# The last 15 of 63 full loads through GpSimd's queue in a row-mean kernel

## The chip, the cores and the metric

The kernel runs on one core of one Trainium2 chip. The metric is the time of one execution on the device in microseconds; three timed runs of the kernel before gave 1243.21, 1243.28 and 1243.29 us. The profile is of one execution, and its span runs from the first to the last instruction.

## The reference

The input `x` has 64 x 256 x 8192 float32 numbers, 536.9 MB. The result is the mean over the last axis, 64 x 256 numbers:

```python
def reference(x):
    return np.mean(x, axis=2)
```

Each of the 16384 rows of 8192 numbers is summed and multiplied by 1/8192. Every number is read once, and almost nothing is written.

## The kernel before

The 16384 rows lie as 128 partitions with 128 rows each. The rows are cut into three zones of 95, 17 and 16 rows per partition (`ZONE`, L27); within a zone a partition owns consecutive rows, so a partition's part of a load is one stretch of memory. A full load takes two rows of each partition, 128 x 16384 numbers or 8 MiB, 64 KB for each partition. There are 63 of them (`NB`, L30), numbered g = 0 to 62; load 0 comes in three pieces. A last pair of rows is the tail: it comes in five chunks that become smaller (`cuts`, L42).

Three buffers of 8 MiB (`bufs`, L67) are used in turn: load g goes to buffer g mod 3. For each buffer there is a semaphore that counts landings (`in_sems`) and one that counts reductions done (`free_sems`). The engines do this:

- SP (`nc.sync`, from L102) issues every transfer, all through its one hardware queue. After the first three loads it runs a loop of 15 rounds of three (`ROUNDS`, L116 to L121): wait until the buffer's reduction is done, issue the load into it. That covers loads 3 to 47. Loads 48 to 62 (L122 to L125) are written out with the same wait. At L126 SP waits until load 60 is reduced, since the tail uses buffer 0, and issues the five chunks (L128 to L131). At the end it writes the results out (L133 to L138).
- DVE (`nc.vector`, from L145) waits for a buffer's landing and sums its two rows with one `tensor_reduce` (L166, in a loop of 20 rounds of three, loads 0 to 59; L176, loads 60 and 61). Load 62 and the tail's first chunk are summed by the helper `halves` (L147 to L158), which adds the two halves of a row and sums the result in one pass; of the chunks DVE sums a part, then adds all the parts of the last row (L197).
- ACT (L200 to L205) sums the other part of the first four chunks.
- GpSimd, POOL in the profile (L87 to L99), clears one cell at the start and multiplies the finished sums by 1/8192 once load 62 and the first chunk are summed.

The order of the loads in SP's queue is the order in which DVE sums them, and no more than three loads can be out or unread at a time.

Of the kernel before, what the change touches and what calls it, by code (L numbers as in the profile page):

```python
# [11 lines left out]
def bass_global_avg_pool_1d_kernel(  # L12
    nc: bass.Bass,
    x: bass.AP,
    out: bass.AP,
):
    P = 128
    ALIGN = 4096
    B, C, L = x.shape
    rows = B * C  # L20
    inv = 1.0 / float(L)

    OWN = rows // P
    ZONE = [95, 17, 16]  # L27
    FROM = [0, ZONE[0], ZONE[0] + ZONE[1]]
    EARLY, LATE = FROM[2], ZONE[2]
    NB = OWN // 2 - 1  # L30
    NBUF = 3
    PAIRS0 = ZONE[0] // 2
    ROUNDS = PAIRS0 // NBUF
    assert rows % P == 0 and sum(ZONE) == OWN and NB % NBUF == 0
    assert ZONE[0] % 2 == 1 and ZONE[1] % 2 == 1
    assert (PAIRS0 + 1) % NBUF == 0 and NB - PAIRS0 - 1 > NBUF
    LOADS0 = (NB - PAIRS0 - 1) // NBUF
    first_row = lambda g: 2 * g - 2 if g <= PAIRS0 else 2 * g
    FIRST = L // 4


    U = L // 256  # L42
    cuts = [0, L + 29 * U, L + 169 * U, L + 217 * U, L + 240 * U, 2 * L]
    mine = [29 * U, 50 * U, 17 * U, 8 * U]
    LAST = cuts[5] - cuts[4]
    NPART = 8

    flat = x.rearrange("b c l -> (b c) l")
    out_flat = out.rearrange("b c -> (b c)")
    zone = [  # L50
        flat[P * f : P * (f + n), :].rearrange("(p r) l -> p (r l)", p=P)
        for f, n in zip(FROM, ZONE)
    ]
    out_zone = [
        out_flat[P * f : P * (f + n)].rearrange("(p r) -> p r", p=P)
        for f, n in zip(FROM, ZONE)
    ]

    with ExitStack() as ctx:
        sb = lambda n, s: ctx.enter_context(nc.sbuf_tensor(n, s, F32))  # L60
        sem = lambda n: ctx.enter_context(nc.semaphore(n))
        res = sb("res", [P, OWN - 1])
        scaled = sb("scaled", [P, EARLY])
        ends = sb("ends", [P, LATE])
        fin = sb("fin", [P, LAST + NPART])
        sb("pad", [P, (-nc.sbuf_base % ALIGN) // 4])
        bufs = [sb(f"buf{i}", [P, 2 * L]) for i in range(NBUF)]  # L67

        in_sems = [sem(f"in_sem{i}") for i in range(NBUF)]
        free_sems = [sem(f"free_sem{i}") for i in range(NBUF)]  # L70
        first_sem = sem("first_sem")
        mixed_sem = sem("mixed_sem")
        chunk_sems = [sem(f"chunk_sem{c}") for c in range(5)]
        owned_sem = sem("owned_sem")
        part_d = sem("part_d")
        part_a = sem("part_a")
        pool_sem = sem("pool_sem")
        late_sem = sem("late_sem")
        out_sem = sem("out_sem")
        end_sem = sem("end_sem")  # L80

        tail = bufs[0]
        part = lambda n: fin[:, LAST + n : LAST + n + 1]

        eng = nc.gpsimd  # L87
        eng.memset(part(NPART - 1), 0.0).then_inc(part_d, 1)  # L88
        eng.wait_ge(free_sems[0], LOADS0 + 1)
        eng.wait_ge(owned_sem, 4)  # L90
        for dst, src in [
            (scaled[:, 0 : ZONE[0] - 1], res[:, 2 : ZONE[0] + 1]),
            (scaled[:, ZONE[0] - 1 : ZONE[0] + 1], res[:, 0:2]),
            (scaled[:, ZONE[0] + 1 : EARLY], res[:, ZONE[0] + 1 : EARLY]),
            (ends[:, 0 : LATE - 1], res[:, EARLY : OWN - 1]),
        ]:
            eng.tensor_scalar(dst, src, inv, None, op0=mybir.AluOpType.mult).then_inc(  # L97
                pool_sem, 1
            )  # L99


        eng = nc.sync  # L102
        def rows_of(n, k):
            z = 2 if n >= FROM[2] else 1 if n >= FROM[1] else 0
            return zone[z][:, (n - FROM[z]) * L : (n - FROM[z] + k) * L]

        a, z = rows_of(ZONE[0] - 1, 1), rows_of(ZONE[0], 1)
        eng.dma_start(bufs[0][:, 0:FIRST], a[:, 0:FIRST]).then_inc(first_sem, 16)
        eng.dma_start(bufs[0][:, FIRST:L], a[:, FIRST:L]).then_inc(mixed_sem, 16)
        eng.dma_start(bufs[0][:, L : 2 * L], z).then_inc(in_sems[0], 16)  # L110
        for g in range(1, NBUF):
            eng.dma_start(bufs[g][:], rows_of(first_row(g), 2)).then_inc(in_sems[g], 16)
        src = rows_of(first_row(NBUF), ROUNDS * NBUF * 2).rearrange(
            "p (i b w) -> b p i w", i=ROUNDS, b=NBUF
        )
        with eng.Fori(0, ROUNDS) as i:  # L116
            for b in range(NBUF):
                eng.wait_ge(free_sems[b], 1).then_inc(free_sems[b], -1)
                eng.dma_start(bufs[b][:], src[b][:, bass.ds(i, 1), :]).then_inc(
                    in_sems[b], 16  # L120
                )  # L121
        for g in range(PAIRS0 + 1, NB):  # L122
            b = g % NBUF
            eng.wait_ge(free_sems[b], (g - PAIRS0 - 1) // NBUF + 1)
            eng.dma_start(bufs[b][:], rows_of(first_row(g), 2)).then_inc(in_sems[b], 16)  # L125
        eng.wait_ge(free_sems[0], LOADS0 + 1)  # L126
        two = rows_of(2 * NB, 2)
        for c in range(5):  # L128
            a, z = cuts[c], cuts[c + 1]
            dst = tail[:, a:z] if c < 4 else fin[:, 0:LAST]  # L130
            eng.dma_start(dst, two[:, a:z]).then_inc(chunk_sems[c], 16)  # L131
        eng.wait_ge(pool_sem, 4)
        for z in range(2):  # L133
            eng.dma_start(
                out_zone[z], scaled[:, FROM[z] : FROM[z] + ZONE[z]]
            ).then_inc(out_sem, 16)
        eng.wait_ge(late_sem, 1)
        eng.dma_start(out_zone[2], ends[:]).then_inc(end_sem, 16)  # L138
        eng.wait_ge(out_sem, 32)
        eng.wait_ge(end_sem, 16)  # L140

        eng = nc.vector  # L145

        def halves(ap, to, done, scale=1.0):  # L147
            n = ap.shape[1] // 2
            eng.tensor_tensor_reduce(  # L149
                ap[:, 0:n],  # L150
                ap[:, 0:n],
                ap[:, n : 2 * n],
                scale=scale,
                scalar=0.0,
                op0=ADD,
                op1=ADD,
                accum_out=to,
            ).then_inc(done, 1)  # L158

        eng.wait_ge(first_sem, 16)  # L160
        eng.wait_ge(mixed_sem, 16)
        sums = res[:, 0 : 2 * (NB - NBUF)].rearrange("p (i b j) -> p i b j", b=NBUF, j=2)
        with eng.Fori(0, NB // NBUF - 1) as i:
            for b in range(NBUF):
                eng.wait_ge(in_sems[b], 16).then_inc(in_sems[b], -16)  # L165
                eng.tensor_reduce(  # L166
                    sums[:, bass.ds(i, 1), b, :],
                    bufs[b][:].rearrange("p (j l) -> p j l", j=2),
                    X,
                    ADD,  # L170
                ).then_inc(free_sems[b], 1)
        for b in range(NBUF):
            g = NB - NBUF + b
            eng.wait_ge(in_sems[b], 16)
            if b < 2:
                eng.tensor_reduce(  # L176
                    res[:, 2 * g : 2 * g + 2],
                    bufs[b][:].rearrange("p (j l) -> p j l", j=2),
                    X,
                    ADD,  # L180
                ).then_inc(free_sems[0] if b == 0 else owned_sem, 1)
            else:
                for j in range(2):
                    halves(
                        bufs[b][:, j * L : (j + 1) * L],
                        res[:, 2 * g + j : 2 * g + j + 1],
                        owned_sem,
                    )
        eng.wait_ge(chunk_sems[0], 16)
        halves(tail[:, 0:L], res[:, 2 * NB : 2 * NB + 1], owned_sem)  # L190
        for c in range(1, 4):
            eng.wait_ge(chunk_sems[c], 16)
            halves(tail[:, cuts[c] + mine[c] : cuts[c + 1]], part(3 + c), part_d)
        eng.wait_ge(chunk_sems[4], 16)
        eng.wait_ge(part_a, 4)
        eng.wait_ge(part_d, 4)
        halves(fin, ends[:, LATE - 1 : LATE], late_sem, inv)  # L197


        eng = nc.scalar  # L200
        for c in range(4):
            eng.wait_ge(chunk_sems[c], 16)
            a = cuts[c] if c else L
            ap = tail[:, a : a + mine[c]]
            eng.activation(ap, ap, COPY, accum_out=part(c)).then_inc(part_a, 1)  # L205
# [28 lines left out]
```

## Time and profile before

| what | value |
|---|---|
| time of the three runs, median | 1243.28 us |
| span of the profiled execution | 1241.9 us |
| instructions in the profile | 549 |
| DVE busy | 1084.1 us, 76 instructions |
| ACT busy | 5.2 us, 9 instructions |
| POOL busy | 2.9 us, 9 instructions |
| read from HBM | 536.87 MB |

The profile gives one span per core and no time of its own for the profiled execution; the median of the runs is 1.4 us above the span. DVE is VectorE, ACT is ScalarE, POOL is GpSimd, SP is SyncE; a name with a q, such as SPq, is the engine's queue, where its waits and its issues of DMA stand. A row of a group gives line, engine, operation, output and input with their shapes, the count, the busy time and the mean duration of one in ns, and the idle time of the engine ahead of them with what ended it. A row of the timeline gives start and duration in us, then the instruction, and in brackets the idle time before it and what ended that. In the list of issues stands the median time from issue to landing. L166 is line 166 of the kernel before.

### The profile page before, as it was taken

What the parts mean: (1) busy time and instruction counts of PE and PEld (TensorE: products, weight loads), DVE (VectorE), ACT (ScalarE), POOL (GpSimd) and SP (SyncE); (2) the same over time, 40 slices, a digit from 0 to 9 for tenths busy, and PEclk for the clock granted to TensorE, in tenths of its full rate; (3) what the DMA queues carried; (4) which work ended last, traced back from release to release, by engine and by line L of the source; (5) the groups of instructions that cost most, each with busy time, mean ns of one, the idle gap of its engine ahead of it and who ended that gap; (6) DMA issues with size and microseconds to landing.
All of it is one profiled execution on the core that took longest, in us unless ns stands there. A gap on an engine that the chain in (4) does not pass through costs nothing. (4 is left out here: it accounts for less than half of the span.)

```text
span 1241.9 us, 549 instructions
## 1 busy us (share of the span) xinstructions
DVE 1084.1 (87%) x76; ACT 5.2 (0%) x9; POOL 2.9 (0%) x9
## 2 busy tenths in 40 slices
DVE  2898988989889898898898988989889898898987
ACT  0000000000000000000000000000000000000001
POOL 0000000000000000000000000000000000000000
DMA  9999999999999999999999999999999999999998
GB/s 405 439 439 439 439 431 414 439 439 439 439 439 431 414 439 439 439 439 439 431 414 439 439 439 439 439 429 416 439 439 439 439 439 429 416 439 439 439 439 374
DMA packets 10512, 536.94 MB, mean 432 GB/s; under 512 B 1552, under 2 KB 1552, under 8 KB 1936
## 3 DMA queue, kind: packets, MB, share of 16 engines
q1 hardware_dynamic: 10512, 536.94, 99.8%
HBM read 536.87 MB, written 0.07 MB: 432 GB/s over the span
## 5 line engine op out<-in xcount | busy, mean ns | idle before, releaser
L166 DVE TENSOR_REDUCE res<-buf 128x16384 f32 x60 | 1033.2, 17220 | 146.7 <-DVEq L165 146.7
L176 DVE TENSOR_REDUCE res<-buf 128x2 f32<-128x16384 f32 x2 | 34.4, 17220 | 4.0 <-DMA buf<-in_x_dram 4.0
L149 DVE CUSTOM_DVE_ANT_0 buf<-buf 128x4096 f32<-128x4096 f32 (+3 forms) x6 | 15.9, 2671 | 5.4 <-DMA buf<-in_x_dram 5.4
L205 ACT ACTIVATE buf<-buf 128x928 f32<-128x928 f32 (+3 forms) x4 | 3.6, 897 | 1233.9 <-DMA buf<-in_x_dram 1233.9
L97 POOL TENSOR_SCALAR scaled<-res 128x94 f32<-128x94 f32 (+2 forms) x3 | 2.4, 784 | 1235.1 <-DVE res L149 1235.0
L205 ACT ACT_TABLE_LOAD x1 | 1.3, 1283 | 0.7 <-PEq L219 0.7
L205 ACT ACTIVATION_READ_ACCUMULATOR buf<-buf 128x1 f32 x4 | 0.7, 186 | 0.0
L149 DVE CUSTOM_DVE_ANT_0 fin<-fin 128x260 f32<-128x260 f32 x1 | 0.4, 430 | 0.2 <-DMA fin<-in_x_dram 0.2
L97 POOL TENSOR_SCALAR ends<-res 128x15 f32<-128x15 f32 x1 | 0.3, 262 | 0.1
L149 DVE DVE_READ_ACCUMULATOR2_ANT res<- 128x1 f32 x3 | 0.2, 83 | 0.0
L149 DVE DVE_READ_ACCUMULATOR2_ANT fin<- 128x1 f32 x3 | 0.2, 81 | 0.0
L219 POOL MEMSET const-uint8-127<- 128x1 uint8 x1 | 0.1, 102 | 0.0
L219 POOL MEMSET const-bfloat16-1.0<- 128x1 bf16 x1 | 0.1, 101 | 0.0
L88 POOL MEMSET fin<- 128x1 f32 x1 | 0.1, 98 | 0.3 <-POOLq L219 0.3
L219 POOL MEMSET const-float32-0.0<- 128x1 f32 x1 | 0.1, 98 | 0.2 <-issue 0.2
L219 POOL MEMSET const-float32-1.0<- 128x1 f32 x1 | 0.1, 98 | 0.0
L149 DVE DVE_READ_ACCUMULATOR2_ANT ends<- 128x1 f32 x1 | 0.1, 83 | 0.0
## 6 DMA issues: line engine op xcount, KB each, us to landing
buf<-in_x_dram SPq DMA_DIRECT2D x1, 4560.0 KB, 32.2
buf<-in_x_dram SPq DMA_DIRECT2D x1, 4096.0 KB, 20.7
buf<-in_x_dram SPq DMA_DIRECT2D x1, 3072.0 KB, 11.5
buf<-in_x_dram SPq DMA_DIRECT2D x1, 2240.0 KB, 37.1
buf<-in_x_dram SPq DMA_DIRECT2D x1, 1024.0 KB, 4.7
buf<-in_x_dram SPq DMA_DIRECT2D x62, 40.3
buf<-in_x_dram SPq DMA_DIRECT2D x1, 768.0 KB, 38.5
buf<-in_x_dram SPq DMA_DIRECT2D x1, 368.0 KB, 39.0
```

The source lines that it names most:

```text
L88: eng.memset(part(NPART - 1), 0.0).then_inc(part_d, 1)
L97: eng.tensor_scalar(dst, src, inv, None, op0=mybir.AluOpType.mult).then_inc(pool_sem, 1)
L149: eng.tensor_tensor_reduce(ap[:, 0:n], ap[:, 0:n], ap[:, n : 2 * n], scale=scale, scalar=0.0, op0=ADD, op1=ADD, accum_out=to,).then_inc(do ...
L166: eng.tensor_reduce(sums[:, bass.ds(i, 1), b, :], bufs[b][:].rearrange("p (j l) -> p j l", j=2), X, ADD,).then_inc(free_sems[b], 1)
L176: eng.tensor_reduce(res[:, 2 * g : 2 * g + 2], bufs[b][:].rearrange("p (j l) -> p j l", j=2), X, ADD,).then_inc(free_sems[0] if b == 0 els ...
L205: eng.activation(ap, ap, COPY, accum_out=part(c)).then_inc(part_a, 1)
L219: nc = _bacc.Bacc("TRN2", target_bir_lowering=False, num_devices=1)
```

## The change

Loads 48 to 62 are taken from SP and issued by GpSimd, with the waits that belong to them. [...] The loads that GpSimd issues have semaphores of their own, for landings (`pool_in_sems`) and for buffers that come free (`pool_free_sems`). DVE's loop ends after 15 rounds, at load 44, and the reductions of loads 45 to 61 are written out, with the old or the new semaphores as the issuer demands. SP's wait ahead of the tail's chunks is on a new semaphore too; the chunks stay in SP's queue. Buffers, loads, reductions and their order on DVE are the same.

```diff
+        def rows_of(n, k):
+            z = 2 if n >= FROM[2] else 1 if n >= FROM[1] else 0
+            return zone[z][:, (n - FROM[z]) * L : (n - FROM[z] + k) * L]
+
         eng = nc.gpsimd
         eng.memset(part(NPART - 1), 0.0).then_inc(part_d, 1)
-        eng.wait_ge(free_sems[0], LOADS0 + 1)
+        for g in range(PAIRS0 + 1, NB):
+            b = g % NBUF
+            eng.wait_ge(pool_free_sems[b], (g - PAIRS0 - 1) // NBUF + 1)
+            eng.dma_start(
+                bufs[b][:], rows_of(first_row(g), 2), single_packet=True
+            ).then_inc(pool_in_sems[b], 16)
+        eng.wait_ge(pool_free_sems[0], LOADS0 + 1)
         eng.wait_ge(owned_sem, 4)
...
-        for g in range(PAIRS0 + 1, NB):
-            b = g % NBUF
-            eng.wait_ge(free_sems[b], (g - PAIRS0 - 1) // NBUF + 1)
-            eng.dma_start(bufs[b][:], rows_of(first_row(g), 2)).then_inc(in_sems[b], 16)
-        eng.wait_ge(free_sems[0], LOADS0 + 1)
+        eng.wait_ge(pool_free_sems[0], LOADS0 + 1)
         two = rows_of(2 * NB, 2)
...
-        with eng.Fori(0, NB // NBUF - 1) as i:
+        with eng.Fori(0, ROUNDS) as i:
...
-        for b in range(NBUF):
-            g = NB - NBUF + b
-            eng.wait_ge(in_sems[b], 16)
-            if b < 2:
+        for g in range(ROUNDS * NBUF, NB):
+            b = g % NBUF
+            if g <= PAIRS0:
+                eng.wait_ge(in_sems[b], 16)
+            else:
+                eng.wait_ge(pool_in_sems[b], 16 * ((g - PAIRS0 - 1) // NBUF + 1))
+            if g < NB - 1:
                 eng.tensor_reduce(
...
-                ).then_inc(free_sems[0] if b == 0 else owned_sem, 1)
+                ).then_inc(pool_free_sems[b] if g < NB - 2 else owned_sem, 1)
```

More of the change, by code (lines that the diff above doesn't have):

```diff
@@ L102, in bass_global_avg_pool_1d_kernel @@
         eng = nc.sync
-        def rows_of(n, k):
-            z = 2 if n >= FROM[2] else 1 if n >= FROM[1] else 0
-            return zone[z][:, (n - FROM[z]) * L : (n - FROM[z] + k) * L]
         a, z = rows_of(ZONE[0] - 1, 1), rows_of(ZONE[0], 1)
```

2 lines of the change are left out of this document (added).

## The prediction

> **What bounds the kernel now.** I read the page's busy shares and DMA queue first, then the groups by line, then the timeline around the place where the change begins and around the end, then the issues.
>
> The page of the kernel before, parts 1 to 3 and 5:
> ```profile
> span 1241.9 us, 549 instructions
> DVE 1084.1 (87%) x76; ACT 5.2 (0%) x9; POOL 2.9 (0%) x9
> ...
> DMA packets 10512, 536.94 MB, mean 432 GB/s; under 512 B 1552, under 2 KB 1552, under 8 KB 1936
> ...
> q1 hardware_dynamic: 10512, 536.94, 99.8%
> ...
> L166 DVE TENSOR_REDUCE res<-buf 128x16384 f32 x60 | 1033.2, 17220 | 146.7 <-DVEq L165 146.7
> L176 DVE TENSOR_REDUCE res<-buf 128x2 f32<-128x16384 f32 x2 | 34.4, 17220 | 4.0 <-DMA buf<-in_x_dram 4.0
> ```
> The one DMA queue kept the 16 DMA engines busy for 99.8% of the span. DVE is busy 87% and idle before nearly every reduction. To see the beat I take the timeline from 853 us, where loads 43 to 48 are reduced, and a second one near the end (start, duration, instruction, idle before):
> ```profile
> 853.53 17.22 DVE L166 TENSOR_REDUCE res<-buf 128x16384 f32 x1 [2.06 <-DVEq L165]
> 870.98 19.65 SPq L119 DMA_DIRECT2D buf<-in_x_dram  x2
> 872.85 17.22 DVE L166 TENSOR_REDUCE res<-buf 128x16384 f32 x1 [2.10 <-DVEq L165]
> 892.23 17.22 DVE L166 TENSOR_REDUCE res<-buf 128x16384 f32 x1 [2.15 <-DVEq L165]
> 909.48 38.91 SPq L125 DMA_DIRECT2D buf<-in_x_dram  x3
> 911.53 17.22 DVE L166 TENSOR_REDUCE res<-buf 128x16384 f32 x1 [2.08 <-DVEq L165]
> 930.81 17.22 DVE L166 TENSOR_REDUCE res<-buf 128x16384 f32 x1 [2.06 <-DVEq L165]
> 950.13 17.22 DVE L166 TENSOR_REDUCE res<-buf 128x16384 f32 x1 [2.10 <-DVEq L165]
> ```
> ```profile
> 1162.64 17.22 DVE L166 TENSOR_REDUCE res<-buf 128x16384 f32 x1 [2.07 <-DVEq L165]
> 1181.75 17.22 DVE L176 TENSOR_REDUCE res<-buf 128x2 f32<-128x16384 f32 x1 [1.89 <-DMA buf<-in_x_dram]
> 1199.00 1.75 SPq L131 DMA_DIRECT2D buf<-in_x_dram  x4
> 1200.79 0.43 SPq L131 DMA_DIRECT2D fin<-in_x_dram  x1
> 1201.13 17.22 DVE L176 TENSOR_REDUCE res<-buf 128x2 f32<-128x16384 f32 x1 [2.15 <-DMA buf<-in_x_dram]
> 1220.43 4.43 DVE L149 CUSTOM_DVE_ANT_0 buf<-buf 128x4096 f32<-128x4096 f32 x1 [2.08 <-DMA buf<-in_x_dram]
> ```
> Load 43 is reduced from 853.53 and load 59 from 1162.64: 16 beats of 19.32 us, 8 MiB each, 434 GB/s. A beat is 17.22 us of reduction and 2.1 us in which DVE waits for the next landing. So the bytes are the bound, and the DMA engines may not run empty. The issues show what keeps them full (count, KB, us from issue to landing):
> ```profile
> buf<-in_x_dram SPq DMA_DIRECT2D x1, 1024.0 KB, 4.7
> buf<-in_x_dram SPq DMA_DIRECT2D x62, 40.3
> ```
> A load lands 40.3 us after its issue: the last 2.1 us of the load in flight, then one whole load queued ahead (19.3), then its own 19.3. The order in which the loads are served is the order in which DVE wants them. There are three buffers, so three loads are all that can ever be out.
>
> **The change part by part.** All sums are made against this execution; its span is 1241.9 us and the three timed runs have a median of 1243.28, so 1.4 us lie around the span, and I keep them.
>
> *Issue by GpSimd.* Fifteen issues go from SP to POOL, which has nothing else to do until its four final multiplications. A software issue is not in this trace. It has cover: when a buffer comes free, 2.1 + 19.3 = 21.4 us of queued transfer are ahead. So its cost is nothing up to 21.4 us each, and beyond that whatever is over. Value: 0.
>
> *Bytes and packets.* The same bytes go to the same places. The count of 10512 packets contains 128 for each full load (62 × 128 = 7936 of them, 64 KB each): under the hardware queue each descriptor is a packet of its own, and one of a load's 8 packets on an engine takes 19.32 / 8 = 2.41 us. [...] A gain could only come out of the 0.2% of the span in which the queue's packets did not occupy the engines, 2.5 us in all; the 15 loads' share is 0.6 us. A loss has no row that excludes it: a gap between two packets. I take 0 and keep a rival for it.
>
> *Loops.* DVE's and SP's loops end after 15 rounds and DVE's rest is written out. The idle before the written-out reductions of L176 (1.89 and 2.15) is that of the looped ones (2.06 to 2.15), and it is waiting for DMA that hides either. Value: 0.
>
> *The handover at load 48.* Here is the term that decides. Up to now one queue set the order. Now load 47 waits in SP's hardware queue, complete and not yet begun, when load 48 arrives in another queue, on the same 16 engines. No row of this trace shows two busy queues, so I work out what follows if an engine takes turns between queues, one packet a turn, with the times of the rows above:
> - 909.45: reduction 45 ends, POOL issues load 48. Load 46 has 2.1 us left.
> - about 911.5: the engines are done with 46. At the first or second turn the new queue gets it, and its packet is the whole of its share of load 48, until about 930.8 (or 2.4 later, if one descriptor of 47 went first).
> - 911.53 to 928.75: DVE reduces 46. At 928.8 POOL issues load 49, which stands ready when 48's packet ends.
> - Next turn: one descriptor of 47 (2.4 us), then the whole packet of 49 (19.3 us). Only then do the other descriptors of 47 go. All three have landed at 911.5 + 3 × 19.32 = 969.5, and 47, which DVE wants first, is the last.
> - DVE waits for 47 from 928.75 to 969.5: 40.7 us instead of 2.1.
> - At 969.5 all three buffers are full and unread: nothing can be issued until 47 is reduced, 17.22 us later. To this come the landing's signal and the new issue's way to its first byte. The nearest row is the first load of the kernel: 4.7 us to landing, of which 1 MiB at 434 GB/s takes 2.4, so 2.3 us. The engines stand idle for 17.2 + 2.3 = **19.5 us**. The lower end is 17.2 (a way that costs nothing); for the upper end a software issue may cost POOL another 1.7 us, which is what its longest instruction takes, and that gives 21.2:
> ```profile
> L97 POOL TENSOR_SCALAR scaled<-res 128x16 f32<-128x16 f32 x1 | 1.7, 1672 | 0.1
> ```
> - Then DVE has three full buffers, runs without waits, and gains 2.07 us a load on the DMA until it waits again about nine loads later, before the end. The engines never run empty a second time, but the 19.5 us are not won back: bytes are the bound.
>
> [...]
>
> *The handover back, at the tail's chunks.* At 1199.00 SP issues five chunks in the hardware queue while 61 is finishing and 62 waits in the other. The rows of the end:
> ```profile
> 1231.18 4.43 DVE L149 CUSTOM_DVE_ANT_0 buf<-buf 128x4096 f32<-128x4096 f32 x1 [1.97 <-DMA buf<-in_x_dram]
> 1236.52 1.66 DVE L149 CUSTOM_DVE_ANT_0 buf<-buf 128x1440 f32<-128x1440 f32 x1 [0.91 <-DMA buf<-in_x_dram]
> 1238.41 0.68 DVE L149 CUSTOM_DVE_ANT_0 buf<-buf 128x496 f32<-128x496 f32 x1 [0.23 <-DMA buf<-in_x_dram]
> 1239.33 0.41 DVE L149 CUSTOM_DVE_ANT_0 buf<-buf 128x240 f32<-128x240 f32 x1 [0.22 <-DMA buf<-in_x_dram]
> 1239.97 0.43 DVE L149 CUSTOM_DVE_ANT_0 fin<-fin 128x260 f32<-128x260 f32 x1 [0.23 <-DMA fin<-in_x_dram]
> 1240.44 0.33 SPq L138 DMA_DIRECT2D out_dram<-ends  x1
> ```
> ```profile
> buf<-in_x_dram SPq DMA_DIRECT2D x1, 4560.0 KB, 32.2
> ```
> The first chunk is this issue, 35.6 KB for a partition, 1.34 us of an engine for a descriptor. With turns by packet one such descriptor goes ahead of 62's packet. DVE then begins 62 at 1221.7, needs 2 × 4.43, and is done at 1230.6; the first chunk lands at 1231.18 as before. It is hidden, with 0.6 us to spare. Value: 0.
>
> Sum: 1243.28 + 19.5 = **1262.8 us**.
>
> **The rivals.**
>
> *The order holds (not slower).* If an engine stays with a queue as long as that has work, 47 goes before 48 and 62 before the chunks, and nothing changes: 1243.3. The same comes out if load 48 reaches the engines only after 47 has gone: the point is 21.4 us after its issue. For it speaks that nothing is removed and all issues have cover; against it, that all descriptors of 47 are there to be overtaken and that 21.4 us are nine times the 2.3 us of the first load.
>
> *Descriptors held up by DVE (not slower, or barely).* If a software issue could not be written while DVE reduces, load 48 would come at 928.75 if the 2.1 us of idle time don't do, the order would hold, and each load would come 2.1 us before the engines run dry, against 2.3 needed: at most 14 × 0.2 = 2.8 us, 1246. [...]
>
> *The eight descriptors do not act as one packet.* Then 47 and 48 alternate, 47 lands near 947.7, is reduced by 965, and load 50 arrives while 49 still runs until 969.5: no idle. At the end the chunk's eight descriptors alternate with 62's: 62 lands 8 × 1.34 = 10.7 us later, at 1231.2, and DVE has everything still to do: 2 × 4.43 + 4.43 + 1.66 + 0.68 + 0.41 + 0.43 and five times some 0.1 for reading the sums, to 1248. That is 7.5 us: 1250.8.
>
> *The hardware queue goes first.* Nothing happens at 48, but all chunks pass 62, which lands at 1239.9. The same DVE work follows it, 17 us: 1259.6.
>
> *A gap at each packet.* If the engines wait at each new packet for as long as at the kernel's first load, 14 × 2.3 = 32 us come on top of the forecast: 1295.
>
> **How the numbers follow.** Turns by packet, 1262.8: 0.66. The order holds: 0.08, with descriptors held up 0.02. Turns by descriptor, 1250.8: 0.10. Hardware first, 1259.6: 0.07. Gaps: 0.06. Some gain beyond the 0.6 us: 0.01. A measurement of this kernel can tell about 0.2%, 2.5 us, from no change. Faster is then 0.01, the same 0.10, slower 0.89. The range leaves out the 0.11 of no change or gain, the 0.06 of gaps and a little of the forecast: it runs from just under turns by descriptor, 1249, to the forecast's upper end, 1243.3 + 21.2 = 1264.5, with 1.5 us for a still slower software issue, 1266.
>
> **What would show it.** DVE should have one wait of about 40 us, ahead of load 47 (the third written-out reduction), and after it some nine reductions with no idle time. The slices of DMA should show one hole of about 19 us near 970 to 989 us, and the loads of the new queue should be landing 19.3 us after their first byte otherwise. The idle before the reduction of 62 should be 1.3 us longer, the end after the last landing unchanged. If DVE's waits near 930 stay at 2.1 us, the turns by packet are wrong; if the wait is near 19 us and DVE comes late to the chunks, packets are not held together; if DVE waits some 20 us ahead of 62, the hardware queue has precedence; if the beat of the last loads is longer than 19.32 us, the new queue costs at each load.

## The result and the profile after

The changed kernel takes 1251.66 us (1251.36 to 1251.67), the kernel before 1243.24 us beside it: a ratio of 1.0067, with a 95% interval from 1.0055 to 1.0079. It is slower by 8.4 us where 19.5 were forecast.

Of the page of the changed kernel, the parts that were shown of the kernel before:
```profile
span 1250.0 us, 504 instructions
DVE 1083.1 (87%) x76; ACT 5.2 (0%) x9; POOL 11.2 (1%) x24
...
q1 hardware_dynamic: 8352, 411.11, 76.0%
q0 software_dynamic: 2160, 125.83, 23.2%
...
L170 DVE TENSOR_REDUCE res<-buf 128x16384 f32 x45 | 774.9, 17220 | 115.2 <-DVEq L169 115.2
L183 DVE TENSOR_REDUCE res<-buf 128x2 f32<-128x16384 f32 x17 | 292.1, 17215 | 36.2 <-DMA buf<-in_x_dram 36.2
...
L98 POOL DMA_DIRECT2D buf<-in_x_dram x15 | 8.1, 539 | 1171.5 <-DVE res L183 1171.5
```
The new queue is there as `software_dynamic`, the software queue of this text, and its count answers the main question: 2160 packets. Each load has 16 signals of its landing, 15 x 16 = 240; the other 1920 are 128 for a load, just as many as in the hardware queue. A packet of eight descriptors, which the forecast took for the new queue, is not seen: with the flag `single_packet=True` each of a load's 128 stretches of 64 KB was a packet of its own. A software issue holds POOL for 0.54 us on the mean. Seven of them, from 965.03 to 1067.79 us, fell into a stretch in which DVE reduced without a pause, and took 0.53 us.

The timeline at the first handover (start, duration, instruction, idle before it):
```profile
891.99 17.22 DVE L183 TENSOR_REDUCE res<-buf 128x2 f32<-128x16384 f32 x1 [1.94 <-DMA buf<-in_x_dram]
909.52 0.71 POOL L98 DMA_DIRECT2D buf<-in_x_dram  x1 [908.69 <-DVE res L183]
911.30 17.22 DVE L183 TENSOR_REDUCE res<-buf 128x2 f32<-128x16384 f32 x1 [2.09 <-DMA buf<-in_x_dram]
928.83 0.53 POOL L98 DMA_DIRECT2D buf<-in_x_dram  x1 [18.60 <-DVE res L183]
947.52 137.10 DVE L183 TENSOR_REDUCE res<-buf 128x2 f32<-128x16384 f32 x8 [19.00 <-DMA buf<-in_x_dram]
965.03 0.53 POOL L98 DMA_DIRECT2D buf<-in_x_dram  x1 [35.67 <-DVE res L183]
...
1085.13 17.22 DVE L183 TENSOR_REDUCE res<-buf 128x2 f32<-128x16384 f32 x1 [0.51 <-DMA buf<-in_x_dram]
1102.65 0.53 POOL L98 DMA_DIRECT2D buf<-in_x_dram  x1 [17.20 <-DVE res L183]
1104.45 17.22 DVE L183 TENSOR_REDUCE res<-buf 128x2 f32<-128x16384 f32 x1 [2.10 <-DMA buf<-in_x_dram]
```
DVE waits 19.0 us ahead of load 47, then reduces eight loads without a pause, and from load 55 on it waits again for landings. Load 50 is issued at 965.03, 3.5 us before the first engine is done with load 49 (968.54 in the trace's packets), so the engines never run empty. The proof is the beat's place: load 56 begins at 1104.45 here; in the kernel before the reduction of that load began at 1104.68. Not a microsecond is lost up to here.

The timeline at the end:
```profile
1181.73 17.22 DVE L183 TENSOR_REDUCE res<-buf 128x2 f32<-128x16384 f32 x1 [2.10 <-DMA buf<-in_x_dram]
1198.97 1.76 SPq L135 DMA_DIRECT2D buf<-in_x_dram  x4
1200.78 0.43 SPq L135 DMA_DIRECT2D fin<-in_x_dram  x1
1201.09 17.22 DVE L183 TENSOR_REDUCE res<-buf 128x2 f32<-128x16384 f32 x1 [2.15 <-DMA buf<-in_x_dram]
1231.18 4.42 DVE L153 CUSTOM_DVE_ANT_0 buf<-buf 128x4096 f32<-128x4096 f32 x1 [12.87 <-DMA buf<-in_x_dram]
...
1244.49 2.48 POOL L109 TENSOR_SCALAR scaled<-res 128x94 f32<-128x94 f32 x3 [64.04 <-DVE res L153]
...
1247.04 0.43 DVE L153 CUSTOM_DVE_ANT_0 fin<-fin 128x260 f32<-128x260 f32 x1 [0.18 <-DVE fin L153]
...
1247.62 0.82 SPq L138 DMA_DIRECT2D out_dram<-scaled  x2
1248.49 0.43 SPq L142 DMA_DIRECT2D out_dram<-ends  x1
```
Up to 1201.09 all stands as before. Then load 62 lands at 1231.18 instead of 1220.43, 10.75 us late. The trace's packets show why: the eight 64 KB packets that an engine has of load 62 begin 3.76 us apart, 2.42 for the packet itself and 1.34 for one of the first chunk's that stands behind it. The signal of 62's landing is a packet too, and it stands behind the eighth: on each engine it begins 1.34 us after the end of the load's last packet, at 1229.3 to 1230.8 us. DVE has 62, the first chunk and all that follows still to do, without a wait, and begins its last addition 7.1 us later than before (1247.04 against 1239.97). One more microsecond comes from the outputs: POOL could multiply only after that late first chunk, SP issues the two early outputs at 1247.62, and the last output, ready at 1247.5, stands behind them until 1248.49. That is 8.05 us after its time of before, 1240.44; 7.1 + 1.0 is the 8.1 us by which the span grew.

### The profile page after: what moved, and what is told of

The parts are those of the page before. It is cut to its first block, busy times and chain, and to the rows that moved or that the text cites. A ratio compares the mean times of both kernels' runs of the same rounds, so it can differ in the third digit from the quotient of the medians.

```text
span 1250.0 us, 504 instructions
## 1 busy us (share of the span) xinstructions
DVE 1083.1 (87%) x76; ACT 5.2 (0%) x9; POOL 11.2 (1%) x24
## 3 DMA queue, kind: packets, MB, share of 16 engines
q1 hardware_dynamic: 8352, 411.11, 76.0%
q0 software_dynamic: 2160, 125.83, 23.2%
## 5 line engine op out<-in xcount | busy, mean ns | idle before, releaser
L170 DVE TENSOR_REDUCE res<-buf 128x16384 f32 x45 | 774.9, 17220 | 115.2 <-DVEq L169 115.2
L183 DVE TENSOR_REDUCE res<-buf 128x2 f32<-128x16384 f32 x17 | 292.1, 17215 | 36.2 <-DMA buf<-in_x_dram 36.2
L153 DVE CUSTOM_DVE_ANT_0 buf<-buf 128x4096 f32<-128x4096 f32 (+3 forms) x6 | 15.7, 2672 | 12.9 <-DMA buf<-in_x_dram 12.9
L98 POOL DMA_DIRECT2D buf<-in_x_dram x15 | 8.1, 539 | 1171.5 <-DVE res L183 1171.5
```

The source lines that it names most:

```text
L98: eng.dma_start(bufs[b][:], rows_of(first_row(g), 2), single_packet=True).then_inc(pool_in_sems[b], 16)
L153: eng.tensor_tensor_reduce(ap[:, 0:n], ap[:, 0:n], ap[:, n : 2 * n], scale=scale, scalar=0.0, op0=ADD, op1=ADD, accum_out=to,).then_inc(do ...
L170: eng.tensor_reduce(sums[:, bass.ds(i, 1), b, :], bufs[b][:].rearrange("p (j l) -> p j l", j=2), X, ADD,).then_inc(free_sems[b], 1)
L183: eng.tensor_reduce(res[:, 2 * g : 2 * g + 2], bufs[b][:].rearrange("p (j l) -> p j l", j=2), X, ADD,).then_inc(pool_free_sems[b] if g < N ...
```

## The experiments

**Theory A**: an engine takes turns between two queues, but a turn is one 64 KB descriptor, with the flag or without it. The first handover then costs nothing and the whole loss is the alternation of load 62 with the first chunk. The rivals are that the flag does hold a part together, that the first handover costs a part, that turns go by bytes, and that the software queue costs by itself.

**Without the flag.**
```diff
-                bufs[b][:], rows_of(first_row(g), 2), single_packet=True
+                bufs[b][:], rows_of(first_row(g), 2)
```


> The changed kernel without the single-packet flag. Theory A (an engine takes turns between its queues descriptor by descriptor, the flag changes nothing): the same time as the changed kernel, 1251.7 us, with DVE's 19.0 us wait ahead of load 47 and 12.9 us ahead of load 62. Rival (the flag does hold a part of the descriptors together, and this part costs or saves): another wait ahead of 47 and another time, 1 us or more away.

Measured: 1251.6 us (1251.32 to 1251.87). The waits of DVE in this run (total, times, longest):
```profile
DVE res L183 <- DMA buf<-in_x_dram: 36.2, 10, 19.0
DVE buf L153 <- DMA buf<-in_x_dram: 12.9, 1, 12.9
```
The waits are those of the changed kernel to a tenth of a microsecond. At 64 KB for a descriptor the flag changed nothing here.

**The tail in GpSimd's queue.** The wait and the five chunk issues move from SP to GpSimd, behind load 62.
```diff
         eng.wait_ge(pool_free_sems[0], LOADS0 + 1)
...
+        for c in range(5):
...
+            eng.dma_start(dst, two[:, a:z]).then_inc(chunk_sems[c], 16)
         eng.wait_ge(owned_sem, 4)
...
```


> The changed kernel with the tail's five chunks issued by GpSimd too, so that 62 and the chunks stand in one queue. Theory A (the loss is only the alternation of 62 with the first chunk; the handover at 48 is free): DVE still waits 19 us ahead of load 47, the wait ahead of 62 falls from 12.9 to 2.1 us, and the time is 1243.3 to 1243.9. Rival 1 (the handover at 48 costs a part): over 1245. Rival 2 (using the software queue at all costs at the end): stays near 1251.

Measured: 1243.26 us (1243.05 to 1243.40), a ratio to the kernel before of 1.0001, interval 0.9991 to 1.0010. Two rows of its timeline, load 47 with its two followers and load 62:
```profile
947.40 51.47 DVE L182 TENSOR_REDUCE res<-buf 128x2 f32<-128x16384 f32 x3 [18.99 <-DMA buf<-in_x_dram]
...
1220.29 4.43 DVE L152 CUSTOM_DVE_ANT_0 buf<-buf 128x4096 f32<-128x4096 f32 x1 [2.10 <-DMA buf<-in_x_dram]
```
The 19 us wait at the first handover is still there, and the loss is gone. So, to within the interval of 0.1%, that wait cost nothing, the software queue cost nothing, and the 8.4 us belong to the second handover.

**The chunks held back until 62 has landed.**
```diff
         eng.wait_ge(pool_free_sems[0], LOADS0 + 1)
+        eng.wait_ge(pool_in_sems[2], 16 * LOADS0)
         two = rows_of(2 * NB, 2)
```


> The changed kernel, but SP issues the chunks only when load 62 has landed. Theory A: no alternation, 62 lands near 1220.4, then the engines are empty for the way from a landing to a new first byte, some 2.3 us, once: 1243.3 + 2.3 + 0.3 = 1245.9. Rival (the end is late for another reason than the alternation): 1251.7 + 2.3 = 1254.

Measured: 1246.36 us (1246.14 to 1246.53). The first chunk in its timeline:
```profile
1234.22 4.42 DVE L154 CUSTOM_DVE_ANT_0 buf<-buf 128x4096 f32<-128x4096 f32 x1 [4.96 <-DMA buf<-in_x_dram]
```
The order is restored and the loss shrinks to a hole in the stream, which is somewhat larger than expected: the first chunk's reduction begins at 1234.22 instead of 1231.18 in the kernel before, 3.0 us for the way from a landing to a new first byte.

**A second hardware queue.** ACT issues loads 48 to 62 and GpSimd none.
```diff
...
         eng = nc.scalar
+        for g in range(PAIRS0 + 1, NB):
+            b = g % NBUF
+            eng.wait_ge(pool_free_sems[b], (g - PAIRS0 - 1) // NBUF + 1)
+            eng.dma_start(
+                bufs[b][:], rows_of(first_row(g), 2)
+            ).then_inc(pool_in_sems[b], 16)
```


> Loads 48 to 62 issued by ACT through the second hardware queue instead of by GpSimd. Theory A (turns by descriptor between any two queues): 19 us wait ahead of 47, 13 us ahead of 62, 1251.4 us. Rival (the alternation is a trait of the software queue; hardware queues are served in order of arrival): 2.1 us waits and 1243.3.

Measured: 1253.39 us (1252.69 to 1254.11). Its waits of DVE:
```profile
DVE res L177 <- DMA buf<-in_x_dram: 38.4, 10, 21.4
DVE buf L147 <- DMA buf<-in_x_dram: 12.9, 1, 12.9
```
Two hardware queues (q1 with 8352 packets, q10 with ACT's 2160) alternated in the same way, with 12.9 us ahead of load 62 again, so this is no trait of the software queue alone. The wait ahead of 47 is one descriptor (2.4 us) longer: the first packet of load 48 begins at 912.9 us here and at 915.4 in the changed kernel, so 48 has one turn more ahead of 47's landing. The time is 1.7 us above the changed kernel's, which A alone does not explain.

**ACT's queue with the tail in it.** To find the place of those 1.7 us, the chunks were moved to ACT's queue too.
```diff
...
         eng = nc.scalar
...
+        for c in range(5):
...
+            eng.dma_start(dst, two[:, a:z]).then_inc(chunk_sems[c], 16)
```


> Loads 48 to 62 and the chunks all in ACT's hardware queue. Theory A: as with GpSimd's queue, 62 on time and 1243.3. Rival (what made ACT's variant 1.7 us longer than the changed kernel lies at the handover at 48, where the order of the first turn differs): 1245.

Measured: 1245.12 us (1244.09 to 1246.14), ratio 1.0016, interval 1.0006 to 1.0025. The alternation's loss is gone, and some 1.9 us stay. Its timeline where DVE has caught up:
```profile
1105.97 17.22 DVE L171 TENSOR_REDUCE res<-buf 128x2 f32<-128x16384 f32 x1 [1.68 <-DMA buf<-in_x_dram]
```
Load 56 lands 1.5 us later than in the changed kernel, where it was reduced from 1104.45, so most of the time was lost before that point. The trace's packets show the place: load 50, which has to wait until 47 is reduced. That comes one turn later here, so 50 is issued at 967.3 instead of 965.0, and the engines are done with load 49 from 968.5 on. The first packets of 50 begin as late as 969.6 and take up to 3.2 us instead of 2.42; its last packet ends at 989.55 against 988.21 in the changed kernel, 1.3 us later. In the run with ACT's queue before this one it ends at 990.35, 2.1 us later, and load 56 is reduced 2.2 us later. So some engines ran dry for a moment, since the issue had a lead of 1.2 us over the first engine instead of 3.5. That an issue given earlier in ACT's queue loses nothing was not tried.

**The first chunk in two transfers**, a test of the dose: its descriptors are half as long. DVE and ACT wait for both pieces.
```diff
...
+            m = (z - a) // 2
+            if c == 0:
+                eng.dma_start(dst[:, 0:m], two[:, a : a + m]).then_inc(piece_sem, 16)
+                dst, a = dst[:, m : z - a], a + m
             eng.dma_start(dst, two[:, a:z]).then_inc(chunk_sems[c], 16)
...
```


> The changed kernel with the tail's first chunk issued as two transfers of half the width, so that its descriptors on an engine are 16 of 17.8 KB instead of 8 of 35.6 KB. Theory A (one descriptor of each queue in turn, whatever its size): 62 meets 8 descriptors of 0.67 us instead of 1.34, lands 5.4 us late instead of 10.7, near 1225.8, and the time is 1246.3 us. Rival (turns by bytes): 62 lands as in the changed kernel, near 1231, and the time stays 1251.7.

Measured: 1246.14 us (1245.95 to 1247.53). Load 62 in its timeline:
```profile
1225.79 4.42 DVE L158 CUSTOM_DVE_ANT_0 buf<-buf 128x4096 f32<-128x4096 f32 x1 [7.50 <-DMA buf<-in_x_dram]
```
62 lands 5.4 us late instead of 10.75, half the dose. Turns by bytes, which would have left it at 1231, are excluded for this run.

**Smaller descriptors in GpSimd's loads**, with the flag and without it: 32 of 16 KB for an engine.
```diff
-                bufs[b][:], rows_of(first_row(g), 2), single_packet=True
+                bufs[b][:], rows_of(first_row(g), 2), single_packet=True, max_dma_last_dim=16384
```


> The changed kernel, its software loads cut into 16 KB descriptors, 32 on an engine, with the single-packet flag. Theory A (one descriptor in turn, flag or not): 47 meets 8 descriptors of 0.61 us, so DVE's wait ahead of it is about 7 us instead of 19; at the end 62's 32 descriptors meet nearly all of the chunks', 62 lands near 1239 and the time is about 1260. Rival 1 (the flag holds these smaller ones together): a wait of 40 us ahead of 47 and 62 on time. Rival 2 (turns by bytes): 19 us ahead of 47.

> The same as the run with 16 KB descriptors, without the flag. Theory A: the same waits and time as with it, about 7 us ahead of 47 and about 1260. Rival 1 (the flag holds small descriptors): differs from it by 30 us in the wait ahead of 47.

Measured: 1261.29 us with the flag and 1260.71 without it, one run each. Loads 47 and 62 with the flag:
```profile
934.91 34.34 DVE L183 TENSOR_REDUCE res<-buf 128x2 f32<-128x16384 f32 x2 [6.35 <-DMA buf<-in_x_dram]
...
1240.40 4.43 DVE L153 CUSTOM_DVE_ANT_0 buf<-buf 128x4096 f32<-128x4096 f32 x1 [20.47 <-DMA buf<-in_x_dram]
```
Without the flag these waits are 6.35 and 20.48. The queue's count is the same in both runs:
```profile
q0 software_dynamic: 7920, 125.83, 23.3%
```
Less 240 signals that is 512 packets for a load, one for each descriptor of 16 KB. The shorter descriptors in the new queue hurt 47 less (6.35 us instead of 19.0) and 62 more (20.47 us instead of 12.9), by the count of turns, and the flag again changed nothing.

**Small loads beside the stream.** In the kernel before, GpSimd also makes eight small loads, one after the other, in turn with and without the flag.
```diff
...
+        for k in range(8):
+            m = 512 if k < 6 else 128
+            eng.dma_start(
+                small[:, 0:m], flat[P * k : P * (k + 1), 0:m], single_packet=k % 2 == 0
+            ).then_inc(small_sem, 16)
+            eng.wait_ge(small_sem, 16 * (k + 1))
```


> The kernel before, with eight small loads by GpSimd beside the stream of the hardware queue, one after the other, their data unused: six of 2 KB for a partition and two of 512 B, in turn with and without the flag. An engine has 8 descriptors of each and the stream's next 64 KB descriptor always ready. Theory A (one descriptor in turn, flag or not): each small load takes 8 or 9 turns with the stream, some 20 us or more from issue to landing, with and without the flag. Rival (the flag holds descriptors this small together): with the flag some 4 us, without it 20.

Measured: 1247.69 us, one run; the small loads move 1.7 MB more, which at 434 GB/s is 3.9 us of the 4.4 that the run took longer. Each issue's row ends with the wait for the load before it. The third to sixth loads (flag, none, flag, none) and the seventh (512 B, flag) are waited for in these rows:
```profile
39.11 0.54 POOL L93 DMA_DIRECT2D small<-in_x_dram  x1 [16.62 <-DMA small<-in_x_dram]
...
56.63 0.54 POOL L93 DMA_DIRECT2D small<-in_x_dram  x1 [16.98 <-DMA small<-in_x_dram]
...
71.85 0.54 POOL L93 DMA_DIRECT2D small<-in_x_dram  x1 [14.68 <-DMA small<-in_x_dram]
...
86.84 0.53 POOL L93 DMA_DIRECT2D small<-in_x_dram  x1 [14.46 <-DMA small<-in_x_dram]
94.83 0.54 POOL L93 DMA_DIRECT2D small<-in_x_dram  x1 [7.45 <-DMA small<-in_x_dram]
```
With and without the flag the waits are alike, as A said, but all are shorter than the 20 us it gave. The queue's count tells why:
```profile
q0 software_dynamic: 544, 1.70, 0.3%
```
128 of the 544 packets are signals. In the trace each load of 2 KB rows makes 64 packets and each of 512 B rows 16, flag or not. That is 4 KB for a packet, two descriptors of 2 KB or eight of 512 B, and the flag had no part in it. The waits fit turns by packet: an engine has four packets of the fifth load and one of the seventh, and the seventh's wait is 7.2 us shorter, three turns of 2.41. In the kernel with the tail in GpSimd's queue the count goes past 4 KB:
```profile
q0 software_dynamic: 2752, 134.22, 25.0%
```
Less the 2160 of the loads and 80 signals, the five chunks have 512 packets there, where SP's queue gave them 128 each. In the trace the last chunk (descriptors of 2048 B) has 64 packets, and so has the fourth (2944 B): two of its descriptors, 5888 B, make one packet. The other 384 are 128 for each of the first three chunks, whose descriptors have 36480, 17920 and 6144 B. Theory A needs this correction: a turn was a packet, and in the software queue two or eight small descriptors went together in one packet of 4 KB or of 5888 B, while each descriptor of 6144 B and of the larger sizes used here was a packet by itself. Sizes between 5888 and 6144 B were not tried.

**The predicted hole, made by other means.** In the kernel with the tail in GpSimd's queue, load 47 alone is cut into descriptors of 16 KB (SP's loop ends a round earlier, and loads 45 to 47 are written out), so that a turn of the new queue is worth four of 47's.
```diff
...
-        with eng.Fori(0, ROUNDS) as i:
+        with eng.Fori(0, ROUNDS - 1) as i:
...
+        for g in range(ROUNDS * NBUF, PAIRS0 + 1):
+            b = g % NBUF
+            eng.wait_ge(free_sems[b], 1).then_inc(free_sems[b], -1)
+            cut = {"max_dma_last_dim": 16384} if g == PAIRS0 else {}
+            eng.dma_start(bufs[b][:], rows_of(first_row(g), 2), **cut).then_inc(
+                in_sems[b], 16
+            )
```


> The kernel with the tail in GpSimd's queue, but load 47 alone cut into 32 descriptors of 16 KB for an engine, so that a turn of the new queue (64 KB) is four times a turn of 47. This brings about, by the size of a turn, the hole that the prediction expected. Theory A (one descriptor in turn): 16 turns with loads 48 and 49, then the rest; 47 lands last of the three, 911.4 + 3 x 19.32 = 969.4, DVE waits 41 us ahead of it, the DMA engines are empty until a buffer is free again, 17.2 us and the way to a new first byte, and the time is 1243.3 + 19.5 = 1262.8. Rival (the DMA engines or the queue make good for it, or the hole is of another size): under 1255.

Measured: 1263.89 us (1263.83 to 1264.07), ratio 1.0167, interval 1.0150 to 1.0184. Loads 47 and 62 in the timeline, and the stretches from 950 us (start and end, length, DVE busy, ACT busy, POOL busy, clock, DMA share, GB/s):
```profile
969.33 51.47 DVE L189 TENSOR_REDUCE res<-buf 128x2 f32<-128x16384 f32 x3 [40.80 <-DMA buf<-in_x_dram]
...
1241.06 4.43 DVE L159 CUSTOM_DVE_ANT_0 buf<-buf 128x4096 f32<-128x4096 f32 x1 [2.11 <-DMA buf<-in_x_dram]
```
```profile
950.00:969.00 19.00, 0.00 (x0) 0.00 (x0) 0.00 (x0) 1.00 0.98 424
969.00:988.00 19.00, 18.67 (x2) 0.00 (x0) 0.53 (x1) 1.00 0.00 0
988.00:1007.00 19.00, 19.00 (x2) 0.00 (x0) 0.53 (x1) 1.00 1.05 442
```
First DVE stands still for 40.8 us while the engines work, then the engines while DVE works: 47's last packet ends at 969.0 us, and the next packet of data begins at 988.1. Load 62 begins at 1241.06, 20.77 us after its place in the kernel with the tail in the same queue (1220.29): 17.22 for the reduction of 47 and 3.55 for the new start.

No run was faster than the kernel before, which fits a stream without holes: only the beginning and the end are left to gain from.

## Why the prediction was wrong

- **What bounds the kernel**: right. The beat stayed 19.32 us in the new queue, and wherever the stream had no hole and the end no delay the time was 1243.3.
- **Issue by GpSimd, loops, 0 us**: right. 0.5 to 0.7 us for an issue, under cover; the variant with the tail in the same queue came out at 1.0001.
- **Eight descriptors as one packet of 19.3 us**: the sum rests on this, and no run shows such a packet; this is the step that failed. The count of 2160 packets and the runs with and without the flag show one descriptor of 64 KB to a packet, and one to a turn of 2.41 us.
- **The handover at 48, 19.5 us**: wrong by that step. With turns of 2.41 us, 47 was ready for DVE at 947.5 and not at 969.5, 50 was issued while 49 was still on its way, with 3.5 us in hand, and the engines stayed busy. The mechanism itself, three buffers full and the wanted one last, was sound: made by other means, its wait was 40.8 us (40.7 forecast) and its hole 20.8 us (19.5). Short was the price of a new start: 2.3 us were taken, 3.0 and 3.55 measured.
- **The handover back, 0 us**: wrong by the same step. Eight packets of the chunk went ahead of 62's landing, not one, and the whole loss of 8.4 us is here. That the kernel would become slower was therefore right for a wrong reason: the handover that should have cost 19.5 us cost nothing, and the one that should have cost nothing cost 8.4. The direction was luck.
- **The rival of turns by descriptor, 1250.8**: this is what happened, with its numbers nearly to the tenth: 47 at 947.7 (947.5), 62 at 1231.2 (1231.18). Short by 0.9 us: it left out the outputs that queue up behind the late multiplications, 1.0 us. It was given a chance of 0.10, since the flag's name was believed before a row could show it. The measured 1251.66 lies in the stated range of 1249 to 1266 only because its lower end reaches down to this rival; the mechanism of the forecast does not lead there.
- **The rivals of a held order, of hardware first, and of gaps**: excluded by the alternation and by the beat. Loads 50 to 56 were issued by GpSimd while DVE reduced without a pause, in 0.53 us each, and load 56 was there on time, so DVE did not hold them up.

## What to carry to other kernels

The two DMA queues kept no order between them, with GpSimd's as with ACT's: where both had work, an engine alternated packet by packet, and a transfer was delayed by one of the other queue's packets for each of its own (load 62 by 10.75 us with eight packets of 1.34 us, by 5.4 us with packets half as long). In this stream, bound by its bytes, that cost nothing in the middle as long as the engines stayed fed, even with a wait of 19.0 us on the reading engine (ratio 1.0001 with the tail in GpSimd's queue). How near that came to a loss shows ACT's variant, where one turn more for the new queue made the next issue late and 1.3 to 2.1 us were lost. And it cost 8.4 us at the end, where the delayed transfer had work behind it. So keep the last transfers in one queue, in the order in which they are used, and before believing an option's name, look at the count of packets in the profile.

## What the runs showed of the hardware

- The single-packet flag did not change the count of packets at 64 KB (2160 in the software queue) and 16 KB (7920) for a descriptor, nor that of a small load at 2 KB (64) and 512 B (16). The waits were the same at 64 KB and 16 KB; at 2 KB they were 16.6 and 14.7 us with it, 17.0 and 14.5 without. Other sizes were not tried.
- Small descriptors of the software queue went together in one packet: eight of 512 B (16 packets for 128 descriptors), two of 2048 B and two of 2944 B (64 for 128). Those of 6144 B, 17920 B, 36480 B and 64 KB (128 for 128), and of 16 KB (512 for 512), were packets by themselves.
- The signal of a landing was a packet of 4 bytes on each engine, at the end of a load, and it waited for its turn like the others: 47's last packet of data ended at 944.7 us, its signals came at 946.8 to 947.2, and DVE began at 947.5.
- From a landing to new bytes, with an issue in between that waited for it, 3.0 us were lost (SP's issue), and 3.55 with GpSimd's issue after a reduction.
- A load issued 1.2 to 1.3 us before the first engine ran dry (by ACT) came too late for some of the engines, and 1.3 to 2.1 us were lost; one issued 3.5 us before (by GpSimd) lost nothing.
